# Softmax maps left undivided: a ratio of sums on the second map, and the norm's eps times the first sum squared

## The chip, the cores and the metric

The kernel runs on one core of a Trainium2 chip. A core has a matrix engine (TensorE, "PE" in the profile, with its weight loads as "PEld"), a vector engine (VectorE, "DVE"), a scalar engine (ScalarE, "ACT"), GpSimd ("POOL") and a queue that issues most transfers (SyncE, "SP"). Each engine works through its own list of instructions in a fixed order and waits on semaphores. The metric is the device time of one execution in microseconds; a version is judged by the median of several.

## The reference

A trunk of two layers on 512 tokens of width 1024. Each layer normalises the tokens, projects them to queries, keys and values for two groups of heads, adds the output projection of both groups to the residual, and adds a squared-ReLU MLP of width 4096. The change is in the second group, four heads of differential attention, cut here to what matters:

```python
s = jnp.einsum('bhmqd,bhmkd->bhmqk', qblk, kh) * scale       # two maps, m = 0, 1, per head
p = jax.nn.softmax(jnp.where(allowed, s, neg), axis=-1)
attn = p[:, :, 0] - lam * p[:, :, 1]
out = jnp.einsum('bhqk,bhkd->bhqd', attn, vh)                 # 128 values per head
...
df_out = rmsnorm(df_heads, subln_norm[l]) * (1.0 - lambda_init)
# rmsnorm(x, g) = x * rsqrt(mean(x * x) + EPS) * g,  EPS = 1e-6
```

With E0, E1 the exponentials of the two maps and S0, S1 their row sums, attn is E0/S0 - lam*E1/S1. The norm that follows works per head and token, over the 128 values, so a factor common to a token's row falls out of it, but for EPS.

## The kernel before, in words

Everything is held transposed: features on the 128 partitions, the 512 tokens along the free axis. Every dense product is split in three passes (high by high, low by high, high by low; helper `three`, L258 to L260) to get float32 accuracy out of the fp32r matmul. A weight block of 128 x 1024 arrives by transfer into a `raw` tile, ScalarE rounds it to `whi` (L118), VectorE subtracts to get `wlo` (L119). Three raw tiles and two split pairs rotate.

In each layer's first part two generators are interleaved by a planner. `dense` walks the projections in the order of `ORDER` (q and k of differential head 0, its values, head 1, and so on, then the other group), and `attn` walks the attention units. `dense` yields the estimated time of each three-pass group, `attn` the estimated matmul time of each step, and the loop at the end of the layer hands out credit so that attention matmuls are spread between dense ones. `later` holds closures that run once a planned time has come (the rope arithmetic, the copies of k). This fixes the order in which instructions are emitted; a scheduler underneath then orders each engine's list by its own estimates of when inputs are ready. So a change of one engine's work can move other instructions.

A differential head b comes in two units (half 0 and 1), each with two blocks of 128 queries, i = 0..3 over the two. Step one (`s1_df`) makes, for each i, the scores of both maps in PSUM (tiles S0d and S1d, where the digit is the layer; L487 and L488; tag "s" has two banks, one for both maps when the block is at most 256 keys wide, else one each), masks a corner (L527, L531), takes the negated row maximum into the small tile `sm` (L528, L532), and exponentiates on ScalarE with the sum accumulated (L540). A score matmul whose bank is still being read by an earlier exponential waits. Then come, on rows of 128 queries:

```python
nc.vector.reciprocal(sm[:, 4:6], sm[:, 2:4])                                   # L546: 1/S0, 1/S1
nc.vector.tensor_mul(sm[:, 5:6], sm[:, 5:6], nlam[:, l : l + 1])               # L547: -lam/S1
nc.gpsimd.tensor_mul(pr[0], pr[0], sm[:, 4:5].to_broadcast([P, wd]))           # L548: E0/S0, on POOL
nc.vector.scalar_tensor_tensor(out=pr[0], in0=pr[1], scalar=sm[:, 5:6], in1=pr[0], ...)   # L549
```

(widths left out). Step two (`s2`, two units later, LAG2) transposes the weights (tiles T0d, T1d, L568) and splits them (zh, zl, fh, fl; L205, L206). Step three (`s3`, three units later) multiplies with the values into one bank (O0d, O1d) and, after half 1, squares it (`sqo`, L617) and copies it scaled (`os`, L618). `start_norm` then runs `rms_a` for that head: transposes of `sqo`, a sum over the 128 values (L230), times 1/128 plus EPS (L231), the power -0.5 on POOL (L236), and two diagonal matrices (dgh, dgl, on POOL, L241 and L243); `finish` broadcasts them by matmul (`rms_b`, L251 and L252) and multiplies (L648).

POOL also does the rope: for each head, `v1 + u` (L460) and `u1 - v` (L459), 128 x 512 each, on products that VectorE took out of PSUM (`u..k`, L451, and `v..k`, L452). ScalarE rounds the results (h0d2k and the like, L205) and copies parts into the key stack (st0d2k, L446, 32 x 512 each); SP moves the rest (L425). Rounding, key copies, weight splits and exponentials stand in one list on ScalarE, and weight splits, maxima, rope products and L546 to L549 in one list on VectorE.

## Time and profile before

| what | us |
|---|---|
| median of 3 runs | 1233.09 |
| lowest and highest of the 3 | 1231.47, 1233.61 |
| the profiled execution | 1232.63 |
| its span in the profile | 1230.8 |
| PE busy in it | 1196.4 |
| DVE, ACT, POOL busy in it | 683.6, 550.6, 210.9 |

The profiled execution is one execution on the chip; its span lies 1.8 us under its own time, which is 0.46 us under the median. The differential heads of layer 0 fill about 50 to 145 us of the span and those of layer 1 about 645 to 745 us. In timeline rows the columns are start and length in us, engine, line, operation, output<-inputs and shape; a bracket at the end is the engine's idle time before it and what ended it. In window rows they are the stretch, its length, and for each engine the busy time and the number of instructions, then the clock granted to PE, the share of the DMA engines, and GB/s.

### The profile page before, as it was taken

To read this page: it belongs to the slowest core of one execution; us is meant where nothing else is said; L and a number is where in the kernel's file an instruction comes from. 1 tells how busy PE (TensorE), PEld (TensorE's weight loads), DVE (VectorE), ACT (ScalarE), POOL (GpSimd) and SP (SyncE) were. 2 spreads that over 40 slices of the span, in tenths; PEclk is the share of its full clock that TensorE was granted. 3 is DMA by queue.
4 is the path that set the end of the run, shared out by engine and by line. 5 is a ranking of instruction groups with operands and counts; after the bars stand their busy time and mean duration, and the time that the engine had idled before them with its cause. 6 is when DMAs were issued, how large, how long until landed. Compare 5 with 4: busy or idle time off the path is not lost.

```text
span 1230.8 us, 15320 instructions
## 1 busy us (share of the span) xinstructions
PE 1196.4 (97%) x5658; PEld 989.4 (80%) x5658; DVE 683.6 (56%) x1009; ACT 550.6 (45%) x932; POOL 210.9 (17%) x267
## 2 busy tenths in 40 slices
PE   8999999999999999999998999999999999999996
PEld 4777888888888888888887788788888888888886
DVE  6687878765442244443367787887644323444325
ACT  5666566544332134333246765665443221433214
POOL 4223453230000000001123244432200000000002
PEclk9999999999999999999999999999999999999998
DMA  6444444123322323323324343432232233233221
GB/s 198 114 142 121 115 134 122 59 86 103 103 88 101 103 88 101 103 87 102 103 84 141 105 134 107 129 92 84 86 103 99 90 103 95 93 103 91 90 94 69
DMA packets 46890, 128.16 MB, mean 104 GB/s; under 512 B 7264, under 2 KB 10336, under 8 KB 46816
## 3 DMA queue, kind: packets, MB, share of 16 engines
q1 hardware_dynamic: 46672, 127.17, 33.8%
q8 instruction: 45, 0.74, 0.2%
q14 instruction: 29, 0.24, 0.1%
q10 hardware_dynamic: 144, 0.02, 0.0%
HBM read 104.09 MB, written 2.10 MB: 86 GB/s over the span
## 4 chain that ended last, share of the span: by engine, by line
PE 87%; DVE 4%; ACT 3%; POOL 2%; issue 1%; DMA 1%; SPq 0%; DVEq 0%; POOLq 0%; ACTq 0%
PE f L258 19%; PE f L259 19%; PE f L260 19%; PE wo L259 2%; PE wo L258 2%; PE wo L260 2%; DVE wlo L119 1%; PE T1s L568 1%; PE T0s L568 1%; ACT p0d L540 1%; PE O1s L597 0%; PE O0s L597 0%; PE O0s L596 0%; PE O1s L596 0%; PE S1d L487 0%
## 5 line engine op out<-in xcount | busy, mean ns | idle before, releaser
L118 ACT ACTIVATE whi<-raw 128x1024 fp32r<-128x1024 f32 (+2 forms) x200 | 205.1, 1027 | 493.3 <-PE f L259 427.6
L119 DVE TENSOR_TENSOR wlo<-raw,whi 128x1024 fp32r<-128x1024 f32 (+2 forms) x200 | 247.7, 1239 | 151.6 <-ACT whi L118 150.5
L258 PE MATMUL f<-h_hi,whi 128*128 128x512 f32 x512 | 199.4, 389 | 0.0
L260 PE MATMUL f<-h_hi,wlo 128*128 128x512 f32 x512 | 199.2, 389 | 0.0
L259 PE MATMUL f<-h_lo,whi 128*128 128x512 f32 x512 | 199.2, 389 | 0.0
L258 PE MATMUL f<-uh,whi 128*128 128x512 f32 x496 | 192.9, 389 | 0.0
L259 PE MATMUL f<-ul,whi 128*128 128x512 f32 x496 | 192.9, 389 | 0.0
L260 PE MATMUL f<-uh,wlo 128*128 128x512 f32 x496 | 192.9, 389 | 0.0
L771 DVE SCALAR_TENSOR_TENSOR ft<-f,rbc 128x512 f32<-128x512 f32 x64 | 44.3, 692 | 163.9 <-PE f L260 163.0
L258 PEld LDWEIGHTS f<-h_hi,whi 128*128 128x128 f32 x512 | 96.1, 188 | 20.0
L260 PEld LDWEIGHTS f<-h_hi,wlo 128*128 128x128 f32 x512 | 96.1, 188 | 20.0
L259 PEld LDWEIGHTS f<-h_lo,whi 128*128 128x128 f32 x512 | 96.1, 188 | 19.8
L223 POOL TENSOR_TENSOR ssq<-ssq,sq 128x512 f32<-128x512 f32 x28 | 44.5, 1591 | 382.1 <-ACT sq L222 372.7
L260 PEld LDWEIGHTS f<-uh,wlo 128*128 128x128 f32 x496 | 93.1, 188 | 19.5
L258 PEld LDWEIGHTS f<-uh,whi 128*128 128x128 f32 x496 | 93.1, 188 | 19.3
L259 PEld LDWEIGHTS f<-ul,whi 128*128 128x128 f32 x496 | 93.1, 188 | 19.2
L800 DVE TENSOR_TENSOR x<-x,f 128x512 f32<-128x512 f32 x32 | 22.0, 688 | 103.0 <-PE f L260 103.0
L340 POOL TENSOR_TENSOR ssq<-ssq,sqf 128x256 f32<-128x256 f32 x6 | 4.4, 738 | 338.4 <-ACT sqf L338 335.0
L206 DVE TENSOR_TENSOR ul<-fu,uh 128x512 fp32r<-128x512 f32 x64 | 44.1, 692 | 0.4 <-ACT uh L205 0.4
L205 ACT ACTIVATE uh<-fu 128x512 fp32r<-128x512 f32 x64 | 40.6, 634 | 2.0
L772 ACT ACTIVATE fu<-ft 128x512 f32<-128x512 f32 x64 | 39.6, 618 | 1.6 <-DVE ft L771 1.6
L508 POOL TENSOR_TENSOR sig0s<-sig0s,C0s 128x128 f32<-128x128 f32 (+3 forms) x32 | 30.1, 939 | 55.0 <-DVE C0s L505 39.0
(722 smaller groups left out, 2164.9 us busy)
## 6 DMA issues: line engine op xcount, KB each, us to landing
raw<-in_w SPq DMA_DIRECT2D x176, 512.0 KB, 3.4
raw<-in_w SPq DMA_DIRECT2D x16, 448.0 KB, 3.2
x<-in_xT SPq DMA_DIRECT2D x8, 256.0 KB, 4.5
out_xT<-y SPq DMA_DIRECT2D x8, 256.0 KB, 2.4
raw<-in_w SPq DMA_DIRECT2D x8, 128.0 KB, 4.5
cos_t<-in_cos SPq DMA_DIRECT2D x2, 256.0 KB, 4.2
sin_t<-in_sin SPq DMA_DIRECT2D x2, 256.0 KB, 4.3
kl0d0k<-l0d0k SPq DMA_DIRECT2D x8, 64.0 KB, 2.2
```

The lines of the kernel that those rows point to most:

```text
L118: nc.scalar.activation(hi[:, a:b], raw[:, a:b], AF.Copy)
L119: nc.vector.tensor_tensor(out=lo[:, a:b], in0=raw[:, a:b], in1=hi[:, a:b].bitcast(F32), op=ALU.subtract)
L205: nc.scalar.activation(hi, src, AF.Copy)
L206: nc.vector.tensor_tensor(out=lo, in0=src, in1=hi.bitcast(F32), op=ALU.subtract)
L223: eng.tensor_tensor(out=ssq, in0=ssq, in1=sq, op=ALU.add)
L258: nc.tensor.matmul(pt, ah, bh, start=first, stop=False)
L259: nc.tensor.matmul(pt, ah, bl, start=False, stop=False)
L260: nc.tensor.matmul(pt, al, bh, start=False, stop=last)
L508: nc.gpsimd.tensor_mul(sig[:, 0:wd], sig[:, 0:wd], C[:, 1 : wd + 1])
L568: nc.tensor.transpose(pt[:, off : off + P], u["w"][qi][:, kb * P : (kb + 1) * P], ident)
L771: nc.vector.scalar_tensor_tensor(out=t, in0=pt, scalar=0.0, in1=rbc, op0=ALU.max, op1=ALU.mult)
L772: nc.scalar.activation(uu, t, AF.Square)
```

## The change

The division of the first map by S0 is left out, so the weights are S0 times what they were: E0 - lam*(S0/S1)*E1. L546 takes the reciprocal of S1 alone; L547 becomes one VectorE instruction that forms S0 * (-lam) * (1/S1) on 128 x 1; L548, the multiplication of the map on POOL, is gone; L549 stays as it is with the new scalar. S0 of the four query blocks of a head is kept in a tile `top` of 128 x 4 (three rotate), into which the exponentials of the first map accumulate. In `start_norm` a new VectorE instruction makes `floor` = EPS * S0 * S0 (128 x 4, once a head), and in `rms_a` the step at L231 adds `floor` in place of EPS for these heads. The other norms are left as they were.

```diff
--- before.py
+++ after.py
@@ -222,13 +222,17 @@
             nc.scalar.activation(sq, x[:, c, :], AF.Square)
         eng.tensor_tensor(out=ssq, in0=ssq, in1=sq, op=ALU.add)
 
-    def rms_a(src, inv_n, col, name, eng, dgt):
+    def rms_a(src, inv_n, col, name, eng, dgt, floor=None):
         pt = bank("t", "rs_" + name)
         if RST and eng is not nc.gpsimd or RST == 2:
             for j in range(4):
                 nc.tensor.transpose(pt[:, j * P : (j + 1) * P], src[:, j * P : (j + 1) * P], ident)
             nc.vector.tensor_reduce(out=ms, in_=pt.rearrange("p (j f) -> p j f", j=4), axis=AX.X, op=ALU.add)
-            nc.vector.tensor_scalar(out=ms, in0=ms, scalar1=inv_n, scalar2=EPS, op0=ALU.mult, op1=ALU.add)
+            if floor is None:
+                nc.vector.tensor_scalar(out=ms, in0=ms, scalar1=inv_n, scalar2=EPS, op0=ALU.mult, op1=ALU.add)
+            else:
+                nc.vector.scalar_tensor_tensor(
+                    out=ms, in0=ms, scalar=inv_n, in1=floor, op0=ALU.mult, op1=ALU.add)
         else:
             for j in range(4):
                 nc.tensor.matmul(pt[:, j : j + 1], src[:, j * P : (j + 1) * P], ones, start=True, stop=True)
@@ -406,6 +410,7 @@
             stacks = {}
             dgs = {}
             heads = {}
+            tops = {}
 
             later = []
 
@@ -513,10 +518,14 @@
                 b, half = u["b"], u["half"]
                 st = {w: stacks[("d", b, w)] for w in "qk"}
                 u["w"] = []
+                if half == 0:
+                    tops[b] = a3.tile([P, 4], F32, tag="top", name=f"top{l}{b}", bufs=3)
+                top = tops[b]
                 for i in (2 * half, 2 * half + 1):
                     wd = P * (i + 1)
                     nm = f"{l}d{b}{i}"
-                    sm = a3.tile([P, 6], F32, tag="sm", name="sm" + nm, bufs=4)
+                    sm = a3.tile([P, 5], F32, tag="sm", name="sm" + nm, bufs=4)
+                    sums = (top[:, i : i + 1], sm[:, 2:3])
                     pr = []
                     both = bank("s", f"S{nm}") if wd <= 256 else None
                     for m in range(2):
@@ -539,15 +548,16 @@
                                     continue
                                 nc.scalar.activation(
                                     pp[:, 0:wd], ss[:, 0:wd], AF.Exp, bias=sm[:, mm : mm + 1],
-                                    accum_out=sm[:, 2 + mm : 3 + mm])
+                                    accum_out=sums[mm])
                         if m == 0 and both is None:
                             yield max(wd, 256) * 2 * MMC
                     pr = [pp for pp, _ in pr]
-                    nc.vector.reciprocal(sm[:, 4:6], sm[:, 2:4])
-                    nc.vector.tensor_mul(sm[:, 5:6], sm[:, 5:6], nlam[:, l : l + 1])
-                    nc.gpsimd.tensor_mul(pr[0][:, 0:wd], pr[0][:, 0:wd], sm[:, 4:5].to_broadcast([P, wd]))
+                    nc.vector.reciprocal(sm[:, 3:4], sums[1])
                     nc.vector.scalar_tensor_tensor(
-                        out=pr[0][:, 0:wd], in0=pr[1][:, 0:wd], scalar=sm[:, 5:6], in1=pr[0][:, 0:wd],
+                        out=sm[:, 4:5], in0=sums[0], scalar=nlam[:, l : l + 1], in1=sm[:, 3:4],
+                        op0=ALU.mult, op1=ALU.mult)
+                    nc.vector.scalar_tensor_tensor(
+                        out=pr[0][:, 0:wd], in0=pr[1][:, 0:wd], scalar=sm[:, 4:5], in1=pr[0][:, 0:wd],
                         op0=ALU.mult, op1=ALU.add)
                     u["w"].append(pr[0])
                     yield max(wd, 256) * (2 if both is None else 4) * MMC
@@ -638,7 +648,10 @@
 
             def start_norm():
                 b, os_, sqo, rc = late[0]
-                dgs[b] = rms_a(sqo, 1.0 / P, rc, f"d{l}{b}", nc.gpsimd, tr)
+                floor = a3.tile([P, 4], F32, tag="floor", name=f"floor{l}{b}")
+                nc.vector.scalar_tensor_tensor(
+                    out=floor, in0=tops[b], scalar=EPS, in1=tops[b], op0=ALU.mult, op1=ALU.mult)
+                dgs[b] = rms_a(sqo, 1.0 / P, rc, f"d{l}{b}", nc.gpsimd, tr, floor)
                 return 0.43
 
             def finish():
```

In the built kernel 32 multiplications leave POOL's list (16 a layer), 8 instructions join VectorE's, and the lists of TensorE, ScalarE and SP keep their instructions. Some of these stand in another order in the stretches of the differential heads: on TensorE mostly score matmuls one or a few places later or earlier among dense ones; on VectorE rope splits, `wlo` and maxima around L549; on ScalarE, in layer 1, exponentials against key copies and roundings; on SP, in layer 1, one weight load behind the 14 moves of head 3's stacks and another behind two moves.

## The prediction

> **What bounds the kernel now.** I read four views in this order: the busy table, the windows of 25 us, TensorE's own waits, and then the timeline around each wait.
>
> ```profile
> PE 1196.4 (97%) x5658; PEld 989.4 (80%) x5658; DVE 683.6 (56%) x1009; ACT 550.6 (45%) x932; POOL 210.9 (17%) x267
> ...
> 50.00:75.00 25.00, 21.30 (x103) 16.26 (x102) 18.55 (x40) 18.57 (x38) 6.29 (x6) 1.00 0.44 132
> ...
> 300.00:325.00 25.00, 25.00 (x112) 20.67 (x112) 12.87 (x15) 11.10 (x15) 0.00 (x0) 1.00 0.25 85
> ...
> 650.00:675.00 25.00, 22.00 (x101) 17.98 (x100) 18.24 (x45) 16.88 (x40) 6.59 (x7) 0.93 0.39 111
> ...
> PE S0d L487 <- ACT p0d L540: 6.7, 5, 2.2
> PE S1d L487 <- ACT p1d L540: 6.4, 4, 3.0
> ```
>
> TensorE is busy for 1196.4 of 1230.8 us, so 34.4 us of idle time is all that a change on other engines can win. The window at 300 us shows the dense part: 25.00 busy of 25.00, 112 matmuls, 0.223 us from one to the next. There TensorE sets the time and POOL does nothing. In the differential heads (the windows at 50 and 650) 3.70 and 3.00 us are idle. The waits name the cause: score matmuls S0d and S1d wait for an exponential that still reads their bank, 6.7 and 6.4 us, 13.1 together. What the change does to the time is what it does to these 13.1 us, give or take new holes. Whatever TensorE saves there is carried to the end, since from there on it is the engine that sets the time.
>
> **What goes and what comes, by its rows.**
>
> ```profile
> L548 POOL TENSOR_TENSOR p0d<-p0d,sm0d 128x128 f32<-128x128 f32 (+3 forms) x16 | 13.5, 844 | 37.2 <-DVE sm0d L546 32.0 <-PE S0d L488 5.2
> L548 POOL TENSOR_TENSOR p1d<-p1d,sm1d 128x128 f32<-128x128 f32 (+3 forms) x16 | 12.3, 773 | 43.1 <-DVE sm1d L546 35.4 <-PE rs_d L229 4.2 <-DVE S1d L527 3.5
> ...
> L546 DVE RECIPROCAL sm0d<-sm0d x16: 142/163/167, 59.9 to 131.1; 128x2 f32<-128x2 f32 x16
> L547 DVE TENSOR_TENSOR sm0d<-sm0d,nlam x16: 141/182/1118, 60.5 to 132.8; 128x1 f32<-128x1 f32 x16
> ...
> 700.64 0.54 SPq L106 DMA_DIRECT2D raw<-in_w  x1
> 721.01 1.08 ACT L118 ACTIVATE whi<-raw 128x1024 fp32r<-128x1024 f32 x1
> ```
>
> Gone from POOL: 16 multiplications at 844 ns and 16 at 773 ns, 25.8 us of POOL. POOL is 17% busy, so these microseconds buy nothing by themselves; they count only where something on TensorE's chain stood behind them. The reciprocal shrinks from two columns to one; I leave it at its median of 163 ns, bounded by its own 142 and 167. L547 becomes a three-operand instruction of the same 128 x 1; the nearest row is L547 itself, 141 to 1118 ns, median 182, and I take no difference. The eight `floor` instructions are new. Their nearest row is L547 too: 8 x 0.18 = 1.5 us of VectorE, at most 8 x 1.12 = 9 us; both ends stay in the range. VectorE is 56% busy, and a `floor` sits among instructions that wait for exponentials, so I cost it at nothing; were it on the chain each time, it would be 0.18 us a head. The changed addition at L231 keeps its shape and count and is costed like its old form, at zero difference. The moved weight loads on SP: the one that goes behind 14 moves was issued at 700.64 and is first read by the third rounding of a weight after that, at 721.01. At 0.6 us to issue a move (the weight load's own 0.54) it goes out some 9 us later and still has 11 us. Nothing, with those 20 us as the cover.
>
> **Wait by wait, layer 0, head 0 to 1 (call it A).**
>
> ```profile
> 59.89 0.44 PE L487 MATMUL S0d<-st0d0k,st0d0q 128*128 128x384 f32 x1 [1.90 <-ACT p0d L540]
> ...
> 65.54 0.67 DVE L452 TENSOR_TENSOR v0d2k<-p0d2k,sin_t 128x512 f32<-128x512 f32 x1
> 66.51 0.83 POOL L548 TENSOR_TENSOR p0d<-p0d,sm0d 128x384 f32<-128x384 f32 x1
> 67.30 1.30 POOL L459 TENSOR_TENSOR u0d2q<-u0d2q,v0d2k 128x512 f32<-128x512 f32 x1
> 68.63 0.63 ACT L205 ACTIVATE h0d2k<-u0d2q 128x512 fp32r<-128x512 f32 x1 [1.76 <-POOL u0d2q L459]
> 69.17 0.67 ACT L540 ACTIVATE p0d<-S0d,sm0d 128x512 f32<-128x512 f32 x1
> 69.98 0.38 PE L487 MATMUL S0d<-st0d1k,st0d1q 128*128 128x256 f32 x1 [1.32 <-ACT p0d L540]
> ...
> 72.30 1.04 POOL L548 TENSOR_TENSOR p0d<-p0d,sm0d 128x512 f32<-128x512 f32 x1 [3.71 <-DVE sm0d L546]
> 72.58 1.31 DVE L206 TENSOR_TENSOR l0d2k<-v0d2q,h0d2k 128x512 fp32r<-128x512 f32 x1 [0.16 <-ACT h0d2k L205]
> 74.61 0.87 PE L568 MATMUL T0d<-edge,p0d 128*128 128x128 f32 x6 [0.40 <-DVE p0d L549]
> ...
> 656.14 0.44 PE L487 MATMUL S1d<-st1d0k,st1d0q 128*128 128x384 f32 x1 [3.00 <-ACT p1d L540]
> ```
>
> The first wait of each layer (1.90 at 59.89, 3.00 at 656.14) comes before any L548, so those 4.9 us stay. The next one, 1.32 us at 69.98, has POOL in its chain: the rope's u0d2q starts at 67.30 because L548 holds POOL from 66.51, though its input v0d2k was out at 65.54 + 0.67 = 66.21. ScalarE stood idle 1.76 us for it, rounded it (68.63) and only then reached the exponential (69.17) that frees the bank. Without L548 u0d2q starts when the POOL instruction ahead of it ends, at 66.5: 0.8 us earlier, and rounding, exponential and score matmul follow. VectorE, which gets past its own L549s a little sooner, adds perhaps 0.1. The second piece, 0.40 us at 74.61: the transposes waited for L549, which stood on VectorE behind l0d2k, and that took 1.31 us while L548 ran (72.30 for 1.04). In the new list L549 comes ahead of l0d2k, so this wait goes. Together 1.3; but the two exponentials and the weight split after it move up by the 0.9 only, so I take -1.1, with -0.8 and -1.3 as ends. What is late next is ScalarE itself.
>
> **Head 3 of both layers (C in layer 0, F in layer 1).**
>
> ```profile
> 121.39 0.48 DVE L549 SCALAR_TENSOR_TENSOR p0d<-p0d,sm0d,p0d 128x256 f32<-128x256 f32 x1 [0.54 <-POOL p0d L548]
> 121.73 0.70 ACT L618 ACTIVATE os<-O0d,gsub 128x512 f32<-128x512 f32 x1
> 122.51 0.63 ACT L205 ACTIVATE h0s0k<-t0s0k 128x512 fp32r<-128x512 f32 x1
> 123.53 0.69 DVE L206 TENSOR_TENSOR l0s0k<-t0s0k,h0s0k 128x512 fp32r<-128x512 f32 x1
> 125.68 0.50 PE L487 MATMUL S0d<-st0d3k,st0d3q 128*128 128x512 f32 x1 [0.93 <-ACT p0d L540]
> ...
> 721.04 0.48 DVE L549 SCALAR_TENSOR_TENSOR p1d<-p1d,sm1d,p1d 128x256 f32<-128x256 f32 x1 [0.54 <-POOL p1d L548]
> 723.60 0.51 PE L487 MATMUL S1d<-st1d3k,st1d3q 128*128 128x512 f32 x1 [0.52 <-ACT p1d L540]
> ```
>
> L549 at 121.39 stood 0.54 us waiting for L548, and behind it on VectorE the eviction of p0s0k, a `wlo`, l0s0k (123.53) and then the maxima. So the chain could move by 0.54. But l0s0k also needs h0s0k from ScalarE, and that stands behind `os`, which ends at 121.73 + 0.70 = 122.43, 0.08 before h0s0k starts. h0s0k thus moves by about 0.1 and ends near 123.1, so l0s0k starts at 123.15 in place of 123.53. C: -0.4, between 0 (ScalarE's order decides) and -0.54. In layer 1 the same L549 waited the same 0.54, and the wait of TensorE is 0.52; the exponential there stands behind h1s0k, again ScalarE. F: -0.2, between 0 and -0.52.
>
> **Head 2 (B in layer 0, E in layer 1).**
>
> ```profile
> 96.39 1.21 DVE L119 TENSOR_TENSOR wlo<-raw,whi 128x1024 fp32r<-128x1024 f32 x1
> 96.43 2.32 POOL L459 TENSOR_TENSOR u0d3q<-u0d3q,v0d3k 128x512 f32<-128x512 f32 x1
> 102.10 0.50 PE L487 MATMUL S0d<-st0d2k,st0d2q 128*128 128x512 f32 x1 [2.23 <-ACT p0d L540]
> ...
> 696.47 0.69 DVE L452 TENSOR_TENSOR v1d3k<-p1d3k,sin_t 128x512 f32<-128x512 f32 x1 [1.22 <-POOL v1d3q L460]
> 697.25 1.47 POOL L459 TENSOR_TENSOR u1d3q<-u1d3q,v1d3k 128x512 f32<-128x512 f32 x1 [0.23 <-DVE v1d3k L452]
> 697.48 2.31 DVE L119 TENSOR_TENSOR wlo<-raw,whi 128x1024 fp32r<-128x1024 f32 x1
> 698.74 0.63 ACT L205 ACTIVATE h1d3k<-u1d3q 128x512 fp32r<-128x512 f32 x1 [2.44 <-POOL u1d3q L459]
> 699.41 1.91 ACT L446 ACTIVATE st1d3k<-h1d3k 32x512 fp32r<-32x512 f32 x3
> 702.06 0.50 PE L487 MATMUL S1d<-st1d2k,st1d2q 128*128 128x512 f32 x1 [2.07 <-ACT p1d L540]
> ```
>
> Both waits, 2.23 and 2.07 us, are the end of the same chain: rope on POOL, rounding (698.74), three key copies (1.91 us), exponential, score matmul. In layer 0 L548 is not what held u0d3q: it ran 96.43 for 2.32 us, against 1.30 for the rope undisturbed (67.30), because `wlo` on VectorE (two SBUF operands) began at 96.39, 0.04 us before it. The same collision in layer 1 fell the other way: u1d3q began at 697.25, `wlo` at 697.48, and it was `wlo` that took 2.31. The one that begins first runs at full speed, the other waits it out. The change takes no rope and no `wlo` away. In layer 0 the new list has the same order, v0d3k, L547, `wlo`, so the collision stays; TensorE has one dense matmul more ahead of the wait: B -0.2, with -1.1 if u0d3q gets in first. In layer 1 the order changes: L549 now stands before v1d3k, and behind v1d3k only a small memset comes before `wlo`. In the old list L549 filled the gap in which u1d3q could start. `wlo` now follows v1d3k at once, while u1d3q starts 0.1 us after v1d3k's end (697.16 to 697.25), so `wlo` should get in first and u1d3q end 1.1 us later. Against that the new order puts two key copies rather than three ahead of the first exponential (0.63 of the 1.91), and one dense matmul, 0.22, moves ahead of the second score matmul. That makes +0.5 for the first of the two exponentials. Between them the new list puts a rounding of 0.63, which leaves the second one 0.9 to 1.1 late, and TensorE needs both banks. Less the 0.22 and a transpose of `sqo` that also moves ahead, I take E +0.6, between +1.1 and -0.3.
>
> [...]
>
> **Head 1 in layer 1 (D).**
>
> ```profile
> 676.49 0.50 PE L487 MATMUL S1d<-st1d1k,st1d1q 128*128 128x512 f32 x1 [0.79 <-ACT p1d L540]
> ```
>
> The new ScalarE list puts one key copy, 0.63 us, ahead of the exponential that frees this bank, and the new TensorE list puts three dense matmuls, 0.67, ahead of the score matmul. They cancel: D -0.1, between +0.6 and -0.6.
>
> **The sum.** A -1.1, B -0.2, C -0.4, D -0.1, E +0.6, F -0.2: -1.4 us. Against the profiled execution, 1232.63, that is 1231.2, and on the scale of the median, 0.46 higher, 1231.7 us. That is 0.11% below 1233.09. A measurement of this kernel tells a difference from none at about 0.2%, 2.5 us; so I forecast no difference that could be told, on the faster side.
>
> **The rivals.** First, more gain: in both layers u..3q starts ahead of `wlo`. Then B is -1.3 and E -0.3 instead of -0.2 and +0.6: another 2.0 us, -3.4, 1229.7, and 1229.0 with C and F at their ends. For it: the start in layer 0 was lost by 0.04 us, and POOL is no longer busy until just then with L548. Against it: v0d3k's end, not POOL, released u0d3q.
>
> Second, nothing: all of L548 was hidden and ScalarE's order sets every wait. For it: TensorE's list of waits has exponentials, never POOL; against it stands the 1.76 us that ScalarE waited for the rope at 68.63. Time 1233.1.
>
> [...]
>
> **Chances.** The forecast as worked out 0.39; nothing 0.18; both of these are within 0.2%, 0.57. More gain 0.30. Slower 0.13. The forecast's own range is 1230.7 to 1232.9. For 8 in 10 the range reaches down to the first rival's time at 1229.0 and up to the point where the third has just decided, 1235.5; what is left out is part of the third rival and a bigger gain than the rows show.
>
> **What would show it.** Right: POOL near 185 us; the wait before S0d at 69.98 down to about 0.4 and the 0.40 before T0d gone; the first waits still 1.90 and 3.00; in layer 1 `wlo` of normal length beside a u1d3q of over 2 us and a wait of about 2.5. Wrong: u0d3q or u1d3q of 1.3 us with its `wlo` of 2.3; a new wait for `wlo`, zl or a weight transfer in place of the removed ones; waits for exponentials that add up to more than 13.1 us; or any change of the dense part from 200 us on, which has no instruction touched.

## The result, and the profile after

The changed kernel took 1230.18 us, the median of 10 executions (1229.75 to 1233.63), against 1234.14 us for ten of the kernel before: a ratio of 0.9976, with a 95% interval of 0.9967 to 0.9985. The same two kernels measured again, 11 executions of each, gave 0.9995 [0.9985, 1.0004] for the changed one and 1.0004 [0.9996, 1.0013] for the one before, both against 29 shared executions of the kernel before. The two comparisons of one pair differ by 0.2%, so neither is the size of the change. What moves between them is the clock granted to TensorE, which differs from execution to execution:

| mean granted clock of the execution | before: number, mean us | after: number, mean us | difference |
|---|---|---|---|
| 0.991 and 0.992 | 11, 1234.35 | 8, 1233.06 | -1.3 |
| 0.993 | 44, 1232.70 | 4, 1231.19 | -1.5 |
| 0.994 and 0.995 | 10, 1231.62 | 4, 1229.90 | -1.7 |

The table leaves out the clocks that only one of the two kernels had. A line through the executions of all kernels of this document, with a level for each kernel, has 0.8 us for each 0.001 of clock and puts the change at -1.2 us, from 1232.7 to 1231.5 at a clock of 0.993. "At equal clock" below means this line. So the change is worth 1.2 to 1.7 us by this. The 4.0 us between the first two medians are more: the ten executions of the changed kernel had a better clock than the eleven of the second comparison (0.9938 against 0.9921 in the mean), which by the line is 1.3 us, and the clock of the first ten of the kernel before is not on record.

The profiled execution took 1230.04 us, its span 1228.3. Its busy row, the windows of 25 us, and TensorE's waits:

```profile
PE 1194.0 (97%) x5658; PEld 987.5 (80%) x5658; DVE 681.4 (55%) x1017; ACT 551.0 (45%) x932; POOL 188.7 (15%) x235
```
```profile
50.00:75.00 25.00, 22.27 (x104) 17.41 (x103) 17.42 (x42) 18.03 (x38) 2.55 (x2) 0.93 0.44 130
300.00:325.00 25.00, 25.00 (x112) 20.70 (x111) 12.25 (x15) 10.26 (x15) 0.00 (x0) 1.00 0.28 89
650.00:675.00 25.00, 21.21 (x103) 16.90 (x102) 20.01 (x51) 18.19 (x43) 3.44 (x2) 1.00 0.41 127
```
```profile
PE S1d L492 <- ACT p1d L549: 6.7, 3, 3.0
PE S0d L492 <- ACT p0d L549: 5.3, 5, 2.2
```

POOL lost 32 instructions and 22.2 us. That is less than the 25.8 us of L548, since other instructions on POOL took longer (the diagonal matrices `dgld` 1.8 us more in eight, u1d3q 0.8). The dense part at 300 us is as it was, 112 matmuls in 25 us. The waits for exponentials fell from 13.1 to 12.0 us. In the changed kernel the score matmul stands on L492, the exponential on L549, the rope on L464 and L465, and the last of the four small steps on L559.

The single waits, from the timelines of the two (us; a dash where there is none over 0.2). The names are those of the prediction:

| wait of TensorE | before | after | difference | forecast |
|---|---|---|---|---|
| first, layer 0 | 1.90 | 1.97 | +0.1 | 0 |
| A | 1.32 + 0.40 | 0.56 | -1.16 | -1.1 |
| B | 0.33 + 2.23 | 0.23 + 2.17 | -0.16 | -0.2 |
| C | 0.93 | 0.40 | -0.53 | -0.4 |
| first, layer 1 | 3.00 | 3.02 | 0 | 0 |
| D | 0.79 | 0.89 | +0.10 | -0.1 |
| E | 2.07 | 2.77 | +0.70 | +0.6 |
| F | 0.52 | - | -0.52 | -0.2 |
| a weight's rounding, at 75.14 | - | 0.26 | +0.26 | not foreseen |
| vT0w, a transpose at 107.59 | - | 0.55 | +0.55 | not foreseen |

The sum of the differences is -0.7 us. All idle time of TensorE between 50 and 200 us and between 640 and 785 us, small gaps included, went from 17.24 to 16.46 us, -0.8. In the second profile of each kernel the long waits were the same within 0.07 us, though the two executions of the changed kernel differed by 3.3 us: the waits go with the kernel, the clock does not. In the profile of the changed kernel a stretch at half clock (60 to 64 us, last section) lies ahead of A; in the run without the floor, below, there was none at that place, and A was 0.56 us as well.

### The profile page after: what moved, and what is told of

It is laid out like the page before. It is cut to its first block, busy times and chain, and to the rows that moved or that the text cites. A ratio compares the mean times of both kernels' runs of the same rounds, so it can differ in the third digit from the quotient of the medians.

```text
span 1228.3 us, 15247 instructions
## 1 busy us (share of the span) xinstructions
PE 1194.0 (97%) x5658; PEld 987.5 (80%) x5658; DVE 681.4 (55%) x1017; ACT 551.0 (45%) x932; POOL 188.7 (15%) x235
## 4 chain that ended last, share of the span: by engine, by line
PE 88%; DVE 4%; ACT 2%; POOL 2%; issue 2%; DMA 0%; SPq 0%; DVEq 0%; POOLq 0%; ACTq 0%
PE f L264 19%; PE f L263 19%; PE f L262 19%; PE wo L263 2%; PE wo L262 2%; PE wo L264 2%; DVE wlo L119 1%; PE T0s L578 1%; PE T1s L578 1%; PE O1s L607 0%; PE O0s L607 0%; PE O0s L606 0%; PE O1s L606 0%; PE S1d L492 0%; ACT x L345 0%
## 5 line engine op out<-in xcount | busy, mean ns | idle before, releaser
L513 POOL TENSOR_TENSOR sig1s<-sig1s,C1s 128x128 f32<-128x128 f32 (+3 forms) x32 | 30.2, 944 | 56.4 <-DVE C1s L510 42.0
```

The lines of the kernel that those rows point to most:

```text
L513: nc.gpsimd.tensor_mul(sig[:, 0:wd], sig[:, 0:wd], C[:, 1 : wd + 1])
```

## The experiments

### The same pair again

No edit: each kernel once more, to see how far the first ratio holds.

> The kernel before, unchanged, once more, for the granted clock of each execution. In the profile of before TensorE had two stretches of 3.4 us at half clock inside the span (one near 18 us, one near 657 us), in that of the changed kernel one (near 60 us). Theory (the multiplication on POOL held three score matmuls): executions of this kernel and of the changed one that have the same granted clock still differ by 1.5 to 2 us. Rival (the clock only): at the same granted clock they differ by less than 0.5 us, and the whole difference of the medians comes from how many such stretches an execution caught. Ratio to the kernel before: 1.000 by both.

> The changed kernel, unchanged, once more. Theory: ratio 0.998 to 0.9985 to the kernel before (1.8 to 2.5 us), the waits of TensorE as in its first profile: head 2 of layer 1 about 2.8 us, head 3 of layer 1 none, u1d3q over 2 us. Rival (the clock only): the same ratio only where the mean granted clock of its executions is higher; and the same 2.8 us wait, which the clock does not touch.

Measured: 1234.06 us for the kernel before and 1232.63 for the changed one, whose lowest and highest were 1229.27 and 1235.40; the ratios stand above. The ratio expected for the changed kernel, 0.998 to 0.9985, did not come again. In the table above, executions of like clock still differ by 1.3 to 1.7 us, so the rival that it is the clock only (less than 0.5 us) is out, and the 1.5 to 2 us expected are reached at their lower end. One kernel spreads over 6 us, and the spread follows the clock (the last section). From here on a difference of 1 to 2 us is read from the waits and at equal clock, not from a median alone.

### The floor left out

```diff
-                floor = a3.tile([P, 4], F32, tag="floor", name=f"floor{l}{b}")
-                nc.vector.scalar_tensor_tensor(
-                    out=floor, in0=tops[b], scalar=EPS, in1=tops[b], op0=ALU.mult, op1=ALU.mult)
-                dgs[b] = rms_a(sqo, 1.0 / P, rc, f"d{l}{b}", nc.gpsimd, tr, floor)
+                dgs[b] = rms_a(sqo, 1.0 / P, rc, f"d{l}{b}", nc.gpsimd, tr)
```

> The changed kernel without the eight instructions that make eps times the sum squared; the heads' norm adds the plain eps to the undivided squares, so that part of the computation is left out. TensorE's, ScalarE's and POOL's lists stay as they are. Theory: the floor costs nothing, the time is within 0.3 us of the changed kernel at equal clock, and every wait of TensorE in the heads within 0.3 us. Rival (the added instructions sit on the chain at 0.2 us a head or more): 0.8 to 1.5 us faster than the changed kernel.

Measured: 1234.55 us, ratio 1.0010 [1.0001, 1.0019]; at equal clock 1232.0, 0.5 above the changed kernel. Its executions had a low clock, 0.9903 in the mean. The waits of the heads are those of the changed kernel (0.56 for A, 2.17 for B, 0.39 for C, 3.00, 0.87 for D, 2.76 for E); the 0.55 before vT0w is gone, and a wait of 0.25 before a transpose at 179.76 is new. All idle time, counted as above, is 0.4 us less than in the changed kernel, while the line puts the run 0.5 us above it, where within 0.3 was expected. So for a run of so low a clock the line is off by about 1 us. The eight `floor` instructions cost nothing that a run could show, as the prediction took it.

### The multiplication put back alone

A POOL multiplication of the first map stands again where it stood, by another number of the same row (the reciprocal of S1, which is ready at the same place), with everything else of the change kept.

```diff
                         op0=ALU.mult, op1=ALU.mult)
+                    nc.gpsimd.tensor_mul(pr[0][:, 0:wd], pr[0][:, 0:wd], sm[:, 3:4].to_broadcast([P, wd]))
                     nc.vector.scalar_tensor_tensor(
```

> The changed kernel, and the multiplication of the first map is back on POOL between the reciprocal and L549, with no other instruction added: it multiplies by the reciprocal of the second sum, so its result is not the reference's, but its shapes and its place are those of before. The run with the column of ones was 5 us slower than the changed kernel, more than the 1.2 to 1.5 us that taking the multiplication away had won, and it had 32 instructions more on VectorE. Theory (POOL's multiplication held three score matmuls, and small VectorE instructions on the chain cost the rest of those 5 us): the waits of head 0 to 1 and of head 3 come back (together 1.5 to 2.5 us more than in the changed kernel), time 1232 to 1234 us, 1 to 2 us over the changed kernel at equal granted clock. Rival (the multiplication itself cost all of the 5 us): 1236 us or more. Rival (the order of the lists won it, not POOL): within 0.5 us of the changed kernel.

Measured: 1234.76 us, ratio 1.0008 [0.9999, 1.0017]; at equal clock 1233.8, 2.3 above the changed kernel. From the timeline of this kernel, the waits that the prediction traced to L548 and the one that it expected to grow without it (columns: start, length, engine, line, operation, shape, then the idle time before it and what ended it):

```profile
72.04 0.39 PE L492 MATMUL S0d<-st0d1k,st0d1q 128*128 128x256 f32 x1 [1.34 <-ACT p0d L549]
76.73 0.87 PE L579 MATMUL T0d<-edge,p0d 128*128 128x128 f32 x6 [0.47 <-DVE p0d L560]
...
127.93 0.50 PE L492 MATMUL S0d<-st0d3k,st0d3q 128*128 128x512 f32 x1 [1.09 <-ACT p0d L549]
704.30 0.50 PE L492 MATMUL S1d<-st1d2k,st1d2q 128*128 128x512 f32 x1 [2.11 <-ACT p1d L549]
726.21 0.49 PE L492 MATMUL S1d<-st1d3k,st1d3q 128*128 128x512 f32 x1 [0.67 <-ACT p1d L549]
```

A is back at 1.34 + 0.47 (before: 1.32 + 0.40), C at 1.09 (0.93), F at 0.67 (0.52), B has not moved (0.30 + 2.17), and E has fallen back from 2.77 to 2.11 (2.07), with u1d3q again of 1.46 us and its `wlo` of 2.31. So the one POOL instruction carries A, C and F, and its leaving carries E. In TensorE's list the score matmuls of A, C and F stand at the same place in this kernel, the changed one and the one before; the lists of the other engines were not held fixed. The rest of the change, the ratio on VectorE, the smaller tile, the kept sums, was in place here and did not keep these waits away.

The rest is not free where the multiplication stands, though. At equal clock this kernel is 1.1 us slower than the kernel before. Its 32 L556 took 17.7 us, against 12.4 in the changed kernel and 11.7 for the 32 L547, in the same place, of the kernel before. All idle time, counted as above, is 17.7 us, 1.3 above the changed kernel; the other 1.0 of the 2.3 us is not assigned.

### The multiplication with a column of ones

The first form of that experiment made a column of ones on VectorE in each step and multiplied by it; later the same column was made and nothing multiplied. In both the tile `sm` has six columns again. The diff is that of the first form; the second has its first added instruction alone.

```diff
+                    nc.vector.tensor_scalar(
+                        out=sm[:, 5:6], in0=sm[:, 3:4], scalar1=0.0, scalar2=1.0, op0=ALU.mult, op1=ALU.add)
+                    nc.gpsimd.tensor_mul(pr[0][:, 0:wd], pr[0][:, 0:wd], sm[:, 5:6].to_broadcast([P, wd]))
```

> The changed kernel, and for each query block the first map is multiplied on POOL by a column of ones that VectorE makes from the reciprocal (32 more instructions of 128 x 1 on VectorE, about 0.16 us each, and the 32 multiplications back on POOL, waiting for the reciprocal as they did). Theory: the wait before the first score matmul of head 1 in layer 0 is back at 1.0 to 1.4 us, L549 of head 3 waits about 0.5 us for POOL again, and the time is that of the kernel before, ratio 0.999 to 1.001. Rival (the smaller operations and the new order of the lists, not POOL): the ratio stays at 0.998 to 0.9985. Rival (the clock only): no difference from the changed kernel at equal granted clock.

> The changed kernel plus 32 VectorE instructions of 128 x 1 (one behind each exponential's sums, writing a column that nothing reads); no multiplication on POOL. It splits the 5 us that the column of ones together with the multiplication by it cost. If the multiplication costs 2 to 3 us there as it does alone, the small instructions cost the rest: 1233.5 to 1234.5 us at the same clock. If small VectorE instructions are free in these stages, as the eight of the floor were: 1231.5 us, and the same multiplication would have cost 5 us in one place and 2.3 in another.

Measured: 1237.41 us with the multiplication, ratio 1.0037 [1.0025, 1.0049]; 1230.73 us without it, ratio 0.9989 [0.9978, 1.0001]. At equal clock they are 5.2 above and 0.2 below the changed kernel. The small instructions alone cost nothing that shows. The multiplication costs 2.3 us where it can start after the reciprocal and 5.2 where it has to wait for a column that is made after the three-operand step: in the latter A has 0.88 + 0.68, B 0.28 + 2.46, vT0w 1.11, D 1.14, and a wait of 0.96 before a diagonal matmul (rb_d) is new. All idle time, counted as above, is 3.4 us more than in the changed kernel; the other 1.8 are not accounted for. The first expectation, the time of the kernel before, was missed by almost 5 us; of the second the last branch came, 5 us in one place and 2.3 in the other.

### The exponential's table loaded earlier

The first wait of layer 1, 3.0 us, ends with a table load of 1.28 us on ScalarE. Here a small exponential some 20 us earlier takes that load, in layer 1.

```diff
                                 rms_b(rbc, f"a{l}", dgs["a"])
+                                if l:
+                                    nc.scalar.activation(prime, rbc[:, 0:1], AF.Exp)
```

> The changed kernel with one more exponential of 128 x 1 on ScalarE early in layer 1, right behind the broadcast of the norm, so that the 1.28 us table load which now stands in front of the first exponential of layer 1 comes some 20 us earlier, where ScalarE has idle time. If that load lies whole in the first wait of layer 1 (3.0 us): the wait falls to 1.7 us and the time by 1.3 us, and by up to 1.7 us more in those executions in which a stretch of half clock followed that wait. If something else ends last there: the wait stays above 2.5 us.

Measured: 1233.54 us, ratio 1.0005 [0.9996, 1.0014], at equal clock 1231.8, 0.3 above the changed kernel. The wait is 3.07. The load is gone from its place, and from the start of the rounding (h1d1k) to that of the exponential it is 5.17 us in place of 6.47. But the score matmul itself stands earlier in TensorE's list, with six dense matmuls fewer ahead of it (1.3 us at 0.223), and so TensorE waits for it as long as before. The scheduler that orders the lists gave the gain to an earlier position, not to a shorter wait.

### Half of the rope on VectorE

The rope's subtraction, 128 x 512, moves from POOL to VectorE. VectorE gets eight more instructions; the collision of u1d3q with `wlo` can no longer occur.

```diff
-                    nc.gpsimd.tensor_sub(u1, u1, v)
+                    nc.vector.tensor_sub(u1, u1, v)
```

> The changed kernel with one of the two rope instructions, u1 minus v, on VectorE in place of POOL (eight of 128 x 512, about 0.69 us each on VectorE). [...]

Measured: 1220.00 us (1219.07 to 1220.86), ratio 0.9894 [0.9881, 0.9908], at equal clock 10.8 below the changed kernel. That is several times the 1.5 to 3 us that I had estimated for a rope out 1.0 to 1.7 us sooner (about 0.69 us on VectorE, up to 2.33 on POOL). Its waits, from the profile's list:

```profile
PE S1d L492 <- ACT p1d L549: 2.5, 3, 1.2
...
PE S0d L492 <- ACT p0d L549: 0.8, 2, 0.5
```

The waits for exponentials are 3.3 us in place of 12.0; A, C and D are gone, and so is the longer wait of B; the two first waits have shrunk by 1.5 and 1.8 us, to 0.46 and 1.19, and E is 0.68. F, gone in the changed kernel, is back with 0.61. All idle time of TensorE in the two stages, counted as above, is 7.4 us in place of 16.5 (without the transposes of the other heads that the earlier end brings into the window). That is 9.0 of the 10.8; the other 1.8 are not assigned. VectorE was not the worse for it: 679.8 us busy against 681.4, although eight instructions of about 0.69 us were added, 5.5 us. The 32 instructions L556 fell from 12.4 to 8.7 us and the 32 L559 from 20.2 to 17.3 us, with no change of their own: 6.6 us, more than was added.

Why the waits shrank is not one thing. First the chain ahead of the first wait of layer 1, from the timeline of the changed kernel:

```profile
644.76 2.00 DVE L119 TENSOR_TENSOR wlo<-raw,whi 128x1024 fp32r<-128x1024 f32 x1
645.63 2.28 POOL L464 TENSOR_TENSOR u1d1q<-u1d1q,v1d1k 128x512 f32<-128x512 f32 x1
647.94 0.64 ACT L205 ACTIVATE h1d1k<-u1d1q 128x512 fp32r<-128x512 f32 x1 [3.55 <-POOL u1d1q L464]
...
649.92 3.19 ACT L451 ACTIVATE st1d1k<-h1d1k 32x512 fp32r<-32x512 f32 x5
...
655.28 0.45 PE L492 MATMUL S1d<-st1d0k,st1d0q 128*128 128x384 f32 x1 [3.02 <-ACT p1d L549]
```

and the same chain with the subtraction on VectorE:

```profile
641.18 0.68 DVE L464 TENSOR_TENSOR u1d1q<-u1d1q,v1d1k 128x512 f32<-128x512 f32 x1
641.95 0.63 ACT L205 ACTIVATE h1d1k<-u1d1q 128x512 fp32r<-128x512 f32 x1 [3.06 <-DVE u1d1q L464]
...
643.92 2.55 ACT L451 ACTIVATE st1d1k<-h1d1k 32x512 fp32r<-32x512 f32 x4
...
648.63 0.45 PE L492 MATMUL S1d<-st1d0k,st1d0q 128*128 128x384 f32 x1 [1.19 <-ACT p1d L549]
```

With POOL the rope's last step lasts 2.28 us beside `wlo`, on VectorE 0.68, and the rounding follows when it is out. So not only B and E have such a collision ahead of them; the first waits have one as well (in layer 0 u0d1q, 2.29 us). But the lists changed too: one key copy fewer (four in place of five, 0.64 us) follows the rounding, and TensorE has three more dense matmuls (0.67 us) ahead of the score matmul, in layer 0 as well. Of the 1.83 us by which this wait shrank about 0.5 are left for the rope.

Then E, with the subtraction on VectorE; the same place in the changed kernel is shown further below:

```profile
688.95 0.67 DVE L464 TENSOR_TENSOR u1d3q<-u1d3q,v1d3k 128x512 f32<-128x512 f32 x1
688.95 0.58 ACT L549 ACTIVATE p1d<-S1d,sm1d 128x384 f32<-128x384 f32 x1 [2.60 <-DVE sm1d L537]
...
689.65 0.63 ACT L205 ACTIVATE h1d3k<-u1d3q 128x512 fp32r<-128x512 f32 x1
689.67 0.50 PE L492 MATMUL S1d<-st1d2k,st1d2q 128*128 128x512 f32 x1 [0.68 <-ACT p1d L549]
```

Here the exponential that frees the bank stands ahead of the rope's rounding, while in the changed kernel it stands behind the rounding and two key copies. At A and B ScalarE's list has the same new order. So in these three the rope has left the chain, whatever its length. In the changed kernel five of the eight subtractions lasted 2.14 to 2.33 us in place of 1.30, 4.8 us more together; that is about half of the 9.0. The collision, the faster engine and the new order share the gain, and no run holds the order fixed to part them.

### The same with the table load earlier, and in the kernel before

Both edits of the two last sections together, and then the rope's subtraction on VectorE in the kernel before, with its multiplication still on POOL.

> Both of these in one kernel. If they are independent, the gains add: 3 to 4.5 us under the changed kernel at equal granted clock, about 1227 to 1229 us, and fewer half-clock stretches, since no wait of TensorE inside the heads is over 2 us. If VectorE is too full: no better than the one with the early table load alone.

> The kernel before with the rope's subtraction on VectorE in place of POOL; the multiplication of the first map stays on POOL. If the long waits in both kernels come from a rope on POOL beside a weight split on VectorE, the kernel before must gain about as much from this move as the changed one did (11 us): 1220.5 to 1223 us, first waits below 0.6 and 1.3 us, the 1.32 us of head 1 in layer 0 gone although the multiplication is still there. What the change is worth on top is then read from this run against the changed kernel with the same move (1220.0): 0.5 to 1.5 us if the multiplication costs only through the waits of VectorE's sum for it, 2 to 3 us if it costs as much as where it was put back alone (2.3 us). If the gain of 11 us needs the multiplication to be gone too, it comes out at 1225 us or more.

Measured: 1220.25 us for the first, ratio 0.9896 [0.9882, 0.9910], the same as without the earlier load; its first wait of layer 1 is 1.26 us, against 1.19. The kernel before with the move took 1221.92 us, ratio 0.9911 [0.9898, 0.9923]. The move gains it 11 us at the median and 9 at equal clock, so the long waits were never the multiplication's: the first ones are 0.50 and 1.19 us here, and the 1.32 us of head 1 in layer 0 is gone. It does not tell the collision from the new order, since the score matmul of each first wait has three more dense matmuls ahead of it here as well, and at B the exponentials stand ahead of the rounding. On top of the move the change is worth 1.9 us at the median (1221.92 to 1220.00, measured in different comparisons) and 2.7 at equal clock. In waits it is 1.25 (8.67 us of idle time against 7.42); so by the clock it is the second branch of that expectation (2 to 3 us) and by the waits the first (0.5 to 1.5), and the runs do not decide. Here the kernel before has its largest new wait, 1.07 us, before a transpose for which VectorE was late. From its timeline:

```profile
124.79 1.23 DVE L119 TENSOR_TENSOR wlo<-raw,whi 128x1024 fp32r<-128x1024 f32 x1
125.02 1.90 POOL L241 TENSOR_TENSOR dghd<-edge,chi 128x512 fp32r<-128x512 f32 x1 [0.34 <-DVE chi L237]
126.01 0.93 DVE L238 TENSOR_TENSOR clo<-rc,chi 128x4 f32<-128x4 f32 x1
126.86 0.68 DVE L206 TENSOR_TENSOR fl0d<-T0d,fh0d 128x512 fp32r<-128x512 f32 x1
...
127.59 0.66 PE L393 MATMUL vT0u<-edge,tv0u 128*128 128x128 f32 x4 [1.07 <-DVE fl0d L206]
```

It is the same pattern with another POOL instruction: the diagonal `dghd` starts beside `wlo` and lasts 1.90 us in place of 1.04, and the small `clo` behind `wlo` takes 0.93 us in place of 0.15.

### Both halves of the rope on VectorE

```diff
-                    nc.gpsimd.tensor_sub(u1, u1, v)
-                    nc.gpsimd.tensor_add(v1, v1, u)
+                    nc.vector.tensor_sub(u1, u1, v)
+                    nc.vector.tensor_add(v1, v1, u)
```

> The changed kernel with both halves of the rope, subtraction and addition, on VectorE: 16 instructions of about 0.69 us leave POOL altogether. [...] If VectorE's order is what remains, the addition now stands ahead of the roundings and maxima that free the banks, 0.69 us each: waits for the exponentials come back, 1220.5 to 1222 us.

Measured: 1218.73 us (1218.24 to 1219.13), ratio 0.9883 [0.9870, 0.9896]. This is the fastest of all that ran, 14 us below the kernel before and 1.3 below the version with one half moved (1.7 at equal clock; idle time 6.2 us in place of 7.4). That is a little more than the 0.5 to 1 us that I had estimated for the small VectorE instructions beside the addition of 1.29 us; the other branch, waits that come back, did not come. The waits for exponentials in its profile:

```profile
PE S1d L492 <- ACT p1d L549: 0.7, 1, 0.7
PE S0d L492 <- ACT p0d L549: 0.7, 2, 0.4
```

Of the 13.1 us of the kernel before 1.4 are left, and VectorE's busy time, 679.4 us, is again no higher for the eight added instructions.

## Why the prediction was right, and where it was not

**The bound.** Right. The dense part did not change, and what can be seen to have been won or lost, 0.8 us of waits, lies in the heads.

**A, B, C.** Right in size: -1.16, -0.16 and -0.53 against -1.1, -0.2 and -0.4. A's rows are as told. From the timeline of the changed kernel:

```profile
65.54 1.29 POOL L465 TENSOR_TENSOR v0d2q<-v0d2q,u0d2k 128x512 f32<-128x512 f32 x1 [16.67 <-DVE u0d2k L456]
66.79 1.30 POOL L464 TENSOR_TENSOR u0d2q<-u0d2q,v0d2k 128x512 f32<-128x512 f32 x1
68.13 0.64 ACT L205 ACTIVATE h0d2k<-u0d2q 128x512 fp32r<-128x512 f32 x1 [1.00 <-POOL u0d2q L464]
68.67 0.67 ACT L549 ACTIVATE p0d<-S0d,sm0d 128x512 f32<-128x512 f32 x1
69.48 0.39 PE L492 MATMUL S0d<-st0d1k,st0d1q 128*128 128x256 f32 x1 [0.56 <-ACT p0d L549]
```

The rope's two halves follow one another on POOL with nothing between; ScalarE is idle 1.00 us ahead of the rounding in place of 1.76, and the wait before the score matmul falls from 1.32 to 0.56. The 0.40 before the transposes is gone, with 0.26 before a dense matmul shortly behind it, at 75.14, in its place. Putting the multiplication back brought both pieces back.

**D.** A cancellation that left +0.10 in place of -0.1, inside its ends.

**E.** The loss was forecast with its mechanism, +0.6, and it came, +0.70. From the timeline of the changed kernel, with two rows of B first:

```profile
95.64 1.21 DVE L119 TENSOR_TENSOR wlo<-raw,whi 128x1024 fp32r<-128x1024 f32 x1
95.67 2.33 POOL L464 TENSOR_TENSOR u0d3q<-u0d3q,v0d3k 128x512 f32<-128x512 f32 x1 [1.48 <-DVE v0d3k L457]
...
695.11 1.20 DVE L119 TENSOR_TENSOR wlo<-raw,whi 128x1024 fp32r<-128x1024 f32 x1
695.23 2.24 POOL L464 TENSOR_TENSOR u1d3q<-u1d3q,v1d3k 128x512 f32<-128x512 f32 x1 [1.29 <-DVE S1d L536]
...
697.50 0.63 ACT L205 ACTIVATE h1d3k<-u1d3q 128x512 fp32r<-128x512 f32 x1 [3.44 <-POOL u1d3q L464]
698.16 1.27 ACT L451 ACTIVATE st1d3k<-h1d3k 32x512 fp32r<-32x512 f32 x2
699.46 0.58 ACT L549 ACTIVATE p1d<-S1d,sm1d 128x384 f32<-128x384 f32 x1
...
700.18 0.50 PE L492 MATMUL S1d<-st1d2k,st1d2q 128*128 128x512 f32 x1 [2.77 <-ACT p1d L549]
```

`wlo` starts 0.12 us before the rope, keeps its 1.20 us, and the rope takes 2.24 in place of 1.47; two key copies follow instead of three. The first rival, the rope ahead of `wlo` in both layers, is out with these rows and with B's, where u0d3q again lasted over 2.3 us. (Its lower end, 1229.0 "with C and F at their ends", is a slip: these take 0.46 us off 1229.7, which is 1229.2.)

**F.** The mis-sized term: -0.52 in place of -0.2. The step that failed is "the exponential there stands behind h1s0k, again ScalarE": it took ScalarE's own list as standing where it stood. Against TensorE it moved forward. The first row is of the timeline of before, the second of that of after:

```profile
719.97 0.61 ACT L617 ACTIVATE sqo<-O1d 128x512 f32<-128x512 f32 x1
...
717.99 0.60 ACT L627 ACTIVATE sqo<-O1d 128x512 f32<-128x512 f32 x1 [0.77 <-PE O1d L264]
```

In the timeline of before the square `sqo` starts at 719.97, 0.84 us ahead of the head's first score matmul at 720.81, and right behind an exponential; in that of after it starts at 717.99, 1.18 us ahead of the same matmul at 719.17, and ScalarE had already been idle 0.77 us for TensorE. So ScalarE was 0.34 us earlier, and VectorE no longer lost 0.54 us to L548. The exponential that frees the bank started 1.35 us after that matmul in place of 2.06, and the wait went whole; its bound, -0.52, was reached.

**Not foreseen.** Two new waits, 0.55 and 0.26 us, which together take back as much as C and F gave above their forecasts and more. The first is a new collision of POOL with VectorE, which is what the chance of "slower" was for. From the timeline of the changed kernel:

```profile
105.72 1.04 POOL L245 TENSOR_TENSOR dghd<-edge,chi 128x512 fp32r<-128x512 f32 x1 [0.47 <-ACT st0d3k L451]
105.83 0.95 DVE L556 SCALAR_TENSOR_TENSOR sm0d<-top,nlam,sm0d 128x1 f32<-128x1 f32 x1
...
106.77 0.68 DVE L392 TENSOR_TENSOR tv0w<-p0w3v,rbc 128x512 f32<-128x512 f32 x1
...
107.59 0.63 PE L397 MATMUL vT0w<-edge,tv0w 128*128 128x128 f32 x4 [0.55 <-DVE tv0w L392]
```

L556, one number per partition, lasts 0.95 us in place of its median of 0.22: it begins 0.11 us behind POOL's `dghd` and is out at 106.78, `dghd` at 106.76. The eviction behind it on VectorE and the transpose after that are late. Beside it stood not a rope but the norm's diagonal matrix, and as a new wait of TensorE it came once. Without the floor L556 started 0.09 us ahead of `dghd`, lasted 0.21 us, and this wait vanished.

**The sum.** -1.4 us forecast. The six terms together came to -1.57; the two new waits and the first wait of layer 0 took 0.9 back. So it is -0.7 to -0.8 in waits of TensorE, and -1.2 to -1.7 in executions of equal clock. That the latter fit the forecast better than the waits do is luck as far as the runs show: 0.4 us and more of them are assigned to nothing, which is within what the line misses elsewhere. Of the 2.5 us between the two profiled spans the waits explain 0.8. The rest is the clock: besides the stretch at half clock at the end, which both have, the execution before has two (at 19 and 657 us) and the one after has one (at 61 us), worth about 1.3 us by the window rows below; some 0.4 us are not assigned. On the scale of the pooled medians (1232.95 in the 78 executions before whose clock is on record, 1231.58 in 21 after) the change is 0.11%, "no difference that could be told"; in the first comparison alone it was 0.24%, with an interval that leaves "no difference" out. The median measured there, 1230.18, lies below the forecast's own range (1230.7 to 1232.9) and near the 1229.7 of the first rival, whose rows did not come; in part it is so low by the better clock of those ten executions, which the prediction did not reckon with. The upper end of the range for 8 in 10, 1235.5, rests on several new collisions ahead of TensorE, a term that no run shows; in its place the changed kernel showed one, of 0.55 us.

**The step I held fixed.** "The first wait of each layer comes before any L548, so those 4.9 us stay" is right for this change, and it hid the larger fact. I read the collisions of rope and weight split as local to B and E. In the changed kernel five subtractions of over 2.1 us stand ahead of five waits: the two first ones, B, D and E. Moving that one instruction took 9 us of 16.5 away, 3.3 of them at the two first waits, in part because the rope is out sooner and in part by the new order of the lists. My expectation for that run had 1.5 to 3 us in it.

## What to carry to other kernels

An instruction on an engine that is 17% busy is not harmless by that: look at what stands beside it, because five of the eight subtractions on POOL ran beside a `wlo` on VectorE and took about 1 us longer (2.14 to 2.33 in place of 1.30), and each stood ahead of a wait of TensorE. Before taking work off such an engine, try moving what remains there to the engine it collides with; eight or sixteen more instructions cost VectorE no busy time in the changed kernel and won nine to ten times what the change did at equal clock. Then read the new lists before naming the cause: part of that gain came with exponentials that the scheduler had put ahead of other work on ScalarE. And where the granted clock varies, compare executions of equal clock and add up the waits of the bounding engine; medians of ten executions of one kernel differed by 2.5 us here.

## What the runs showed of the hardware that I had not expected

**The clock drops after waits, and not always.** Rows of 2 us, with the clock granted to PE in the third column from the end. The kernel before, after its 3.00 us wait that ends at 656.14:

```profile
658.00:660.00 2.00, 2.00 (x7) 1.52 (x6) 1.90 (x5) 1.93 (x6) 0.02 (x1) 0.50 0.40 100
```

The changed kernel, after its 1.97 us wait that ends at 58.79, and at 656 us, after one of 3.02:

```profile
60.00:62.00 2.00, 2.00 (x7) 1.61 (x7) 2.00 (x6) 0.00 (x0) 0.00 (x0) 0.52 0.27 66
62.00:64.00 2.00, 2.00 (x7) 1.63 (x6) 1.02 (x3) 1.35 (x4) 0.00 (x0) 0.63 0.74 190
...
656.00:658.00 2.00, 2.00 (x10) 1.58 (x9) 1.99 (x9) 1.98 (x6) 0.00 (x0) 1.00 0.39 98
```

And the changed kernel in its second profile, after the wait of E, which had left the clock whole in the first:

```profile
704.00:706.00 2.00, 2.00 (x8) 1.66 (x7) 1.86 (x6) 1.77 (x5) 0.06 (x1) 0.50 0.39 98
```

Read in windows of 0.1 us, the stretches at half clock ahead of the one at the end last 3.4 us each in these two profiles: 18.7 to 22.1 and 657.0 to 660.4 in the kernel before, 60.1 to 63.5 in the changed one. Others are longer: with half of the rope on VectorE the rows of 2 us from 16 to 26 have clocks of 0.85, 0.50, 0.50, 0.50 and 0.94, 6.8 us at half clock, and in the run without the floor those from 700 to 706 have 0.81, 0.50 and 0.50. In the heads a stretch begins during a wait or a little after it: at 657.0 in the kernel before, 0.9 us after the end of its wait; at 60.1 in the changed kernel, 1.3 us after; at 703.2 in its second profile, 1.3 us after the end of E's wait (701.90); and in E's wait itself in the run without the floor, where the row from 700 to 702 with its clock of 0.81 has TensorE busy for 0.08 us. 7 and 7 matmuls at 60 to 64 us, against 10 and 10 in the kernel before at that time, are 6 lost at about 0.22 us, 1.3 us. Which waits are followed by one changes between executions of the same kernel: a wait of 3.02 us had none, one of 1.97 had. What decides it, no run here shows. With half of the rope on VectorE, where the long waits are gone, its profile shows such a stretch only near the start (17 to 25 us) and at the end.

**An instruction recorded first can still be the one that waits.** From the timeline of the changed kernel:

```profile
692.61 1.35 DVE L556 SCALAR_TENSOR_TENSOR sm1d<-top,nlam,sm1d 128x1 f32<-128x1 f32 x1
692.65 1.29 POOL L465 TENSOR_TENSOR v1d3q<-v1d3q,u1d3k 128x512 f32<-128x512 f32 x1 [20.09 <-DVE sm1d L555]
```

The median of L556 is 0.22 us. Here it is recorded 0.04 us ahead of the POOL instruction, lasts 1.35 us and is out at 693.96, 0.02 us after it, while `wlo`, 0.03 us ahead of its rope in B, kept its 1.21 us and the rope took 2.33. So "the one that begins first runs at full speed" does not hold of L556 here: of starts within 0.04 us, these rows show either one waiting for the other.
